# Two-layer hybrid diffusion block on one core: each token mixer starts inside the last group of the mixer before it

## The chip, the cores and the metric

One core of a Trainium2 chip runs the whole program. The metric is device time in microseconds (us), the median of several executions.

## The reference, cut to what matters

Two layers act on 512 latent tokens and, in layer 0, on 256 context tokens as well, each token 1024 wide, in fp32. One layer computes:

```python
hl = rmsnorm(x, ln1_g[l]) * (1.0 + sc1) + sh1
hc = rmsnorm(xc, ln1_g[l]) * (1.0 + csc1) + csh1
zl, zc = hl @ w_in[l], hc @ w_in[l]        # one wide projection, split by columns
ya = hyena_branch(hy)                      # two long convolutions, by DFT matrices here
yb = global_attention_branch(ga)           # 4 heads of 128, qk-norm, axial rotary
yc = mlstm_branch(ml)                      # 4 heads, forward and backward
yd = window_attention_branch(wa)           # 8 heads of 64, band of 128, sink logits
acc = sum(sigmoid(gate[n]) * (ys[n] @ w_up[n]) for n in range(4))
x = x + g1 * (acc @ w_out)
x = x + g2 * sq_relu_mlp(h2, w1, b1, w2, b2)
```

The four branches read the same normed input and do not read each other. Only the sum of the four joins them.

## The kernel before, in words

**Number format.** Most products are done as three fp32r matmuls: an operand is split into a high part H (a cast on ScalarE) and a low part L (a subtraction on VectorE or GpSimd), and H·H, H·L and L·H are summed in PSUM. `load` brings one weight tile of 256 KB (512 rows of 128 columns) from HBM and splits it. Two of these make one projection column block: 24 matmuls of 512 columns, and 24 more of 256 columns where the context tokens take part.

**An order written out by hand.** The program text is made by Python generators ("strands"). A strand emits instructions and yields an estimate of how long it has to wait. `run` steps the main strand when its wait is over on a modelled clock `clk`, and between steps calls `fill_step`, which emits work from three queues: `side` (the Hyena filter spectra), `mods` (blocks of the modulation matrix) and `jobs` (sigmoid gates, `gate_units`, and the gated sum, `merge_units`). This work is called filler below. Every TensorE instruction is chained to the one emitted before it, so TensorE executes exactly in the order of emission; the order on the other engines is settled when the program is built, and a tile that finds no free buffer makes its first writer wait.

**The mixers.** In each layer, four strands run one after the other, each with a `run` of its own: `wa` (window attention), `ga` (global attention), `ml` (mLSTM), `hy` (Hyena). `intake` loads the weights of a list of column blocks, always one block ahead, and projects them; a flag `busy` lets only one intake be under way. A mixer starts with an intake of its first blocks (`wa`, `ga`: k, v and a first q; `ml`: its gate columns, then v, k and q of head 0; `hy`: three channel blocks), has four groups (heads or channel blocks), and within a group `pipe` keeps two steps alive; the intake for the next group is one of the items of the pipe. The last group has no such item. After a mixer, its `merge_units` are added to `jobs`; after `wa`, the loop first empties `side`.

**Buffers.** 17 SBUF tiles of 768 columns (`slot`), 8 of 1024 columns (`big`), 4 raw weight tiles, 6 split weight tiles of each kind. PSUM has three pairs: `p2` (1024 columns, two banks each; projections, scores, transposes), `p1` (512; small sums and outputs), `m` (512; the filler's own). `wa` holds for its whole last group V, four key tiles and two query tiles, and per step one tile for the probabilities and one for their transpose; the output takes two. `ga`'s first intake keeps three tiles for k, one for v and three for q until its norm and rotary (`prep`) are done.

**After the four mixers** `drain` empties the queues, then `last_merge` adds the Hyena branch, followed by the output projection and the MLP.

Of the kernel before, what the change touches and what calls it, by code (L numbers as in the profile page):

```python
# [25 lines left out]
SEQ = 512  # L26
CTX = 256
# [4 lines left out]
HY0, GA0, ML0, WA0, GT0 = 0, 1536, 2560, 4624, 5392  # L32
LAT = (0, SEQ)
CTXS = (SEQ, CTX)
NT, NS = 17, 8
LEAD = 7.0
PACE = {"hy0": 6, "hy1": 2.55, "mlp": 7}
WT = {"wa1": 4.0, "wa2": 1.4, "waq": 6.0, "wak": 3.0, "gap": 3.19, "gaq": 2.0, "ga1": 4.0, "ga2": 1.4, "gas": 6.0,
# [67 lines left out]
def hybrid_block(ctx: ExitStack, tc: tile.TileContext, I, C, out, dbg=None, stop=None):  # L106
# [10 lines left out]
    cnt, ph, clk, last, busy = [0], ["pre"], [0.0], [None], [False]  # L117
# [32 lines left out]
    def acc_tile(segs, filler=False):  # L150

        if filler:
            return [(t0, n, pf1()[:, :n]) for t0, n in segs]
        w, t = span(segs), p2()
        return [(w.start, w.stop - w.start, t[:, w])]
# [189 lines left out]
    def span(segs):  # L345
        a = min(s[0] for s in segs)
        b = max(s[0] + s[1] for s in segs)
        return slice(a, b)
# [359 lines left out]
    def hview(hH, hL):  # L708
        return lambda k: (hH[:, k, :], hL[:, k, :])

    def intake(l, specs, mov, paired=None):

        def weights(col, segs, permute, use):
            w = I["w_in"][l][:, col : col + P]
            return [load((lambda raw, x=x: permute(raw, x)) if permute else wcols(w, x)) for x in range(2)]

        while busy[0]:
            yield 0.4
        busy[0] = True
        ahead = weights(*specs[0])  # L720
        if paired:
            second = weights(*specs[1])
        yield LEAD
        for i, (col, segs, permute, use) in enumerate(specs):
            W = ahead
            if paired and i < 2:
                if i == 0:
                    Ws = W, second
                    ps2 = [acc_tile(t[1]) for t in specs[:2]]
                    yield from paired(ps2, Ws, mov)  # L730
                else:
                    ahead = weights(*specs[2])
                use(ps2[i])
                continue
            if i + 1 < len(specs):
                ahead = weights(*specs[i + 1])
            ps = acc_tile(segs)
            yield from proj(ps, W, mov)
            use(ps)
        busy[0] = False  # L740
# [50 lines left out]
    def window_branch(l, vt, mov, segs, ymk, late, paired):  # L791
# [80 lines left out]
        def next_query(j):  # L872
            yield from intake(l, [query(j)], mov)
            yield WT["waq"]
            Q[j] = stack_q(rope2(*Q[j], segs), segs)
# [53 lines left out]
        for j in range(4):  # L929
            items = [step(j, i, r) for i in range(nblk) for r in range(2)]  # L930
            if j < 3:
                items.insert(3, next_query(j + 1))
            yield from pipe(items)

    def global_branch(l, vt, mov, segs, ymk):
# [59 lines left out]
        def rows(kv, h):  # L995

            yield from intake(l, (key(kv) if kv is not None else []) + [query(h)], mov)
            if kv is not None:
                s, sq, sw, v = K[kv]
                pt = tokens_major(v, full)  # L1000
                V = slot(name="gV")
                nc.vector.tensor_copy(V[:, :TOT], pt[:, :TOT])
                kH, kL, _ = yield from prep(s, sq, sw, full, True)
                K[kv] = kH, kL, V
            else:
                yield WT["gaq"]
            Q[h] = yield from prep(*Q[h], segs, False)
# [41 lines left out]
        for h in range(4):  # L1049
            items = [step(h, i) for i in range(nblk)]  # L1050
            if h < 3:
                items.insert(2, rows(1 if h == 1 else None, h + 1))
            yield from pipe(items)

    def mlstm_branch(l, vt, mov, segs, ymk):
# [10 lines left out]
        for x in range(2):  # L1066
            H, L = (t.rearrange("p k n -> p (k n)") for t in whalf())
            nc.gpsimd.memset(H.bitcast(F32), 0.0)
            nc.gpsimd.memset(L.bitcast(F32), 0.0)
            quad = lambda t: t.rearrange("p (k g c) -> p k g c", k=4, g=4)  # L1070
            low(quad(H)[:, :, :, 0:4], quad(L)[:, :, :, 0:4], quad(raw[:, x * 64 : x * 64 + 64]), heng=nc.vector)
            W.append([t.rearrange("p (k n) -> p k n", k=4) for t in (H, L)])
        pg = acc_tile(full)
        yield from proj(pg, W, mov)
        gb = tiny(8, "gb")
# [239 lines left out]
        yield from pipe([columns(), head(0)])  # L1315
        yield WT["mlh"]
        for h in range(4):
            yield from pipe([mix(h)] + ([head(h + 1)] if h < 3 else []))

    def hyena_branch(l, vt, mov, segs, ymk, near_end):  # L1320
        tabs = {}
        for n in (SEQ, CTX) if CTXS in segs else (SEQ,):
            kt, nb = n // 256, n // P
            fw = [big(name="dft") for _ in range(2)] if n == SEQ else None
            t = big(name="dft") if n == CTX else None
            tv = []
            for j, nm in enumerate(("ap", "am", "tp", "tm")):
                k = kt if j < 2 else nb
                c = n if j < 2 else n // 2
                if n == SEQ:  # L1330
                    b_ = big(name="dft") if j >= 2 else fw[j]
                    v = b_.rearrange("p (k n) -> p k n", k=k)
                else:
                    v = t[:, j * 256 : (j + 1) * 256].rearrange("p (k n) -> p k n", k=k)
                nc.sync.dma_start(v, C[f"{nm}{n}"].rearrange("(k p) n -> p k n", p=P))
                tv.append(v)
            tabs[n] = tv
        w = span(segs)
        U = {}

# [87 lines left out]
                yield WT["hy5"]  # L1428
                U[ct].append(None)

        yield from inputs(0)
        yield WT["hy5"]
        if len(segs) > 1:
            for ct in range(4):
# [49 lines left out]
    def pipe(gens, depth=2):  # L1484

        it, live, more = iter(gens), [], True
        while True:
            while more and len(live) < depth:
                g = next(it, None)
                if g is None:  # L1490
                    more = False
                else:
                    live.append([g, clk[0]])
            if not live:
                return
            e = next((e for e in live if e[1] <= clk[0] + 1e-6), None)
            if e is None:
                yield min(e[1] for e in live) - clk[0]
                continue
            try:  # L1500
                e[1] = next(e[0]) + clk[0]
            except StopIteration:
                live.remove(e)
            yield 0.0
# [26 lines left out]
    def next_fill():  # L1531

        if cur[0] is not None:
            return cur[1]
        return min([q[0].after for q in queues()] + [1e9])
# [11 lines left out]
    def fill_step():  # L1547
# [19 lines left out]
        ph[0] = mine  # L1567
        return True

    def run(lab, gen, pace=0):  # L1570

        ready, i = clk[0], 0
        while True:
            if ready <= clk[0] + 1e-6:
                if WT["eager"] and cur[0] is None and cur[2] is None and side and side[0].after <= clk[0]:
                    fill_step()
                ph[0] = lab
                try:
                    ready = next(gen) + clk[0]
                except StopIteration:  # L1580
                    return
                i += 1
                if pace and i % pace == 0:
                    fill_step()
            elif not fill_step():
                clk[0] = min(ready, max(next_fill(), clk[0] + 0.05))
# [330 lines left out]
    first = []  # L1917
# [26 lines left out]
    for l in range(DEPTH):  # L1944
# [38 lines left out]

        if l == 0:
            first_jobs()
        yds = {}
        for n, lab, branch in ((3, "wa", window_branch), (1, "ga", global_branch), (2, "ml", mlstm_branch),
                               (0, "hy", hyena_branch)):
            yds[n], mk = ymaker(l, n, segs)
            res, extra = [], []  # L1990
            if n == 3:
                extra = [late, by_pieces(full, hdone) if l else by_halves]
            elif n == 0:
                merge = last_merge(l, 0, gd[0], segs, yds[0], res)
                extra = [lambda: next(merge)]
            strand = branch(l, vt, mov, segs, mk, *extra)
            if l and n == 3:
                strand = pipe(before + [then(hdone, full, first_jobs), strand], 9)
            run(f"{lab}{l}", strand, pace=PACE.get(f"{lab}{l}", 0))
            if n == 3 and l == 0:  # L2000
                vturn(False)
            if n == 2 and l == 0:
                vloads(True, nc.sync)
                vloads(False, nc.sync)
            if n == 0 and l == 0:
                vturn1(True)
                vturn1(False)
            while n == 3 and side:
                if not fill_step():
                    clk[0] = max(next_fill(), clk[0] + 0.05)  # L2010
            if n:
                jobs.extend(merge_units(l, n, mov, segs, yds[n], gd.get(n), first=n == 3))
        drain()
        sc2 = mod_scale(l, vt, 4, "ln2_g")
        run(f"mg0x{l}", merge)
# [85 lines left out]
```

## Time and profile before

| | before |
|---|---|
| time, median of 3 runs | 3291.99 us (3285.04 to 3303.0) |
| the profiled execution: its own time | 3282.8 us |
| its span, from first to last instruction | 3281.0 us |
| TensorE matmuls busy (PE) | 3087.7 us, 94% |
| weight loads busy (PEld) | 80% |
| VectorE, ScalarE, GpSimd busy (DVE, ACT, POOL) | 41%, 35%, 42% |
| mean granted TensorE clock, as a share of full speed | 0.976 |

PE is the TensorE matmul queue, PEld its weight loads, SP the queue that issues the transfers. A busy time counts every instruction from start to end; where PE's busy time is close to the window's width, TensorE was never without a matmul. In the view by windows, the width less PE's busy time is its idle time.

### The profile page before, as it was taken

The page shows a single profiled execution, that of the slowest core. Times are in us where ns is not written, and L with a number is a line of the kernel's source. Part 1 is how long each engine was busy: PE and PEld are TensorE (multiplying, and loading weights), DVE is VectorE, ACT ScalarE, POOL GpSimd, SP SyncE. Part 2 cuts the span into 40 slices and gives each one's busy share as a digit, 9 for nine tenths or more (in the row PEclk, how much of TensorE's full clock was granted, in tenths as well). Part 3 has the DMA queues.
Part 4 walks back from the last instruction along what each step waited for, and adds up shares of the span by engine and source line. Part 5 has one row for each costly group of instructions (what it writes and reads, how often), then busy time and mean ns, then how long its engine had stood idle before and what let it go on. Part 6 is the DMA issues. An engine that isn't in the chain of part 4 may idle for free. (4 is left out here: it accounts for less than half of the span.)

```text
span 3281.0 us, 48633 instructions
## 1 busy us (share of the span) xinstructions
PE 3087.7 (94%) x18344; PEld 2614.1 (80%) x18344; DVE 1337.5 (41%) x2892; ACT 1135.7 (35%) x2137; POOL 1384.8 (42%) x1206
## 2 busy tenths in 40 slices
PE   7888989899999999999999997989998999999999
PEld 5777778788888888888888876777777788788887
DVE  6544422454444454511221265434354434442223
ACT  5435423234332122422222254333333432243333
POOL 4523332324344453443333355233333455555553
PEclk8999999999999999999999988999999999999999
DMA  8343443333243456222222334544343343823332
GB/s 269 102 115 114 124 147 94 106 101 95 78 147 92 137 173 198 68 78 75 71 74 75 95 99 121 145 136 113 100 113 98 104 137 116 273 84 97 97 97 81
DMA packets 556922, 380.24 MB, mean 116 GB/s; under 512 B 45177, under 2 KB 503870, under 8 KB 556688
## 3 DMA queue, kind: packets, MB, share of 16 engines
q1 hardware_dynamic: 556056, 376.98, 38.5%
q8 instruction: 145, 2.38, 0.3%
q14 instruction: 89, 0.73, 0.1%
q10 hardware_dynamic: 632, 0.16, 0.0%
HBM read 307.52 MB, written 63.75 MB: 113 GB/s over the span
## 5 line engine op out<-in xcount | busy, mean ns | idle before, releaser
L177 POOL TENSOR_TENSOR mlp__wL<-mlp__raw,mlp__wH 128x512 fp32r<-128x512 f32 x268 | 353.6, 1321 | 457.8 <-ACT mlp__wH L193 324.3
L193 ACT CAST mlp__wH<-mlp__raw 128x512 fp32r<-128x512 f32 x268 | 166.2, 621 | 505.3 <-PE mlp__p L215 340.6
L177 POOL TENSOR_TENSOR gt__wL<-gt__raw,gt__wH 128x512 fp32r<-128x512 f32 x128 | 167.4, 1313 | 240.1 <-ACT gt__wH L193 208.7
L215 PE MATMUL mlp__p<-out__hH,mlp__wH 128*128 128x512 f32 (+1 forms) x760 | 259.5, 353 | 0.5 <-ACT out__hH L518 0.5
L215 PE MATMUL mlp__p<-out__hL,mlp__wH 128*128 128x512 f32 (+1 forms) x760 | 256.5, 352 | 2.0 <-POOL out__hL L516 1.8
L180 DVE SCALAR_TENSOR_TENSOR mlp__x<-mlp__p,modT,mlp__x 128x512 f32<-128x512 f32 (+1 forms) x169 | 106.3, 657 | 338.3 <-PE mlp__p L215 332.1
L215 PE MATMUL mlp__p<-mlp__y,mlp__wH 128*128 128x512 f32 (+1 forms) x672 | 231.9, 356 | 0.0
L215 PE MATMUL mlp__p<-mlp__aL,mlp__wH 128*128 128x512 f32 (+1 forms) x672 | 231.2, 355 | 0.0
L177 DVE TENSOR_TENSOR mlp__aL<-mlp__mq,mlp__y 128x768 fp32r<-128x768 f32 (+1 forms) x64 | 82.4, 1287 | 304.3 <-ACT mlp__y L193 304.1
L215 PE MATMUL gt__m<-mod__hH,gt__wH 128*128 128x512 f32 (+1 forms) x512 | 172.1, 352 | 7.6 <-ACT mod__g L423 3.4
L215 PE MATMUL mlp__p<-out__hH,mlp__wL 128*128 128x512 f32 (+1 forms) x760 | 177.2, 350 | 0.0
L215 PE MATMUL gt__m<-mod__hL,gt__wH 128*128 128x512 f32 (+1 forms) x512 | 166.6, 341 | 0.0
L177 POOL TENSOR_TENSOR ml__wL<-ml__raw,ml__wH 128x512 fp32r<-128x512 f32 x64 | 83.9, 1311 | 189.8 <-ACT ml__wH L193 173.1
L215 PEld LDWEIGHTS mlp__p<-out__hH,mlp__wH 128*128 128x128 f32 x760 | 144.0, 189 | 22.0 <-issue 2.2
L215 PEld LDWEIGHTS mlp__p<-out__hL,mlp__wH 128*128 128x128 f32 x760 | 143.4, 190 | 22.4 <-POOL out__hL L516 2.2
L215 PE MATMUL mlp__p<-mlp__y,mlp__wL 128*128 128x512 f32 (+1 forms) x672 | 155.8, 354 | 0.0
L215 PEld LDWEIGHTS mlp__p<-out__hH,mlp__wL 128*128 128x128 f32 x760 | 130.0, 190 | 18.8
L215 PEld LDWEIGHTS mlp__p<-mlp__y,mlp__wH 128*128 128x128 f32 x672 | 126.8, 189 | 19.9 <-issue 2.2
L215 PEld LDWEIGHTS mlp__p<-mlp__aL,mlp__wH 128*128 128x128 f32 x672 | 127.1, 189 | 18.0
L193 ACT CAST gt__wH<-gt__raw 128x512 fp32r<-128x512 f32 x128 | 79.0, 619 | 173.1 <-DMA gt__raw<-in_w_in_dram 108.0
L215 PEld LDWEIGHTS mlp__p<-mlp__y,mlp__wL 128*128 128x128 f32 x672 | 115.0, 189 | 17.6
L215 PEld LDWEIGHTS gt__m<-mod__hH,gt__wH 128*128 128x128 f32 x512 | 98.3, 192 | 20.9 <-ACT mod__g L423 4.9
(574 smaller groups left out, 7915.5 us busy)
## 6 DMA issues: line engine op xcount, KB each, us to landing
mlp__raw<-in_mlp_w_dram SPq DMA_DIRECT2D x240, 256.0 KB
mod__raw<-in_w_mod_dram SPq DMA_DIRECT2D x160, 256.0 KB
gt__raw<-in_w_in_dram SPq DMA_DIRECT2D x128, 256.0 KB
ml__raw<-in_w_in_dram SPq DMA_DIRECT2D x64, 256.0 KB
hy__raw<-in_w_in_dram SPq DMA_DIRECT2D x48, 256.0 KB
spec<-spec__kk SPq DMA_DIRECT2D x80, 128.0 KB
ga__raw<-in_w_in_dram SPq DMA_DIRECT2D x32, 256.0 KB
hy__spec<-spec SPq DMA_DIRECT2D x16, 512.0 KB
```

The source lines that it names most:

```text
L177: (eng or nc.vector).tensor_tensor(o, a, b, op)
L180: nc.vector.scalar_tensor_tensor(o, a, s, b, op0, op1)
L193: nc.scalar.copy(H, src)
L215: in_order(nc.tensor.matmul(ps, lhsT=a, rhs=b, start=start, stop=stop_), cost)
```

## The change: what it does, and the diff

The four strands of a layer become members of one outer `pipe` of depth 4, in the old order of priority, under a single `run`. Each strand (`mixer`, wrapped in `staged`) polls every 0.3 us of modelled time until its name is in `near`. The mixer before it adds that name by the item `hint`: `wa` as the fourth item of its last group (`NEAR = 3`), `ga` as the third of its last group, `ml` at the start of its last head. From then on both strands are stepped, the earlier one first. `ml` gets a modelled wait (`LEAD`, 7.0) between the load of its gate weights and their projection. Hyena's DFT tables are no longer requested at the start of its strand but by `late_tables`, once `ml` has ended. The emptying of `side` after `wa` becomes a wait of `wa`'s strand alone. The pace at which `run` forces a filler step goes by the mixer that was stepped last. What the fillers load, and how far ahead, stays as it was.

```diff
-NT, NS = 17, 8
+NT, NS, NEAR = 17, 8, 3
...
+    def hint(n):
+
+        near.add(n)
+        yield 0.0
...  (window attention, then global attention, then mLSTM)
             if j < 3:
                 items.insert(3, next_query(j + 1))
+            else:
+                items.insert(NEAR, hint("ga"))
...
             if h < 3:
                 items.insert(2, rows(1 if h == 1 else None, h + 1))
+            else:
+                items.insert(2, hint("ml"))
...
+        yield LEAD
         pg = acc_tile(full)
         yield from proj(pg, W, mov)
...
-            yield from pipe([mix(h)] + ([head(h + 1)] if h < 3 else []))
+            yield from pipe([mix(h)] + ([head(h + 1)] if h < 3 else [hint("hy")]))
...  (Hyena: the loop over the tables becomes tables(n))
+        def late_tables():
+            while "ml" not in ended:
+                yield 0.3
+            for n in (SEQ, CTX) if CTXS in segs else (SEQ,):
+                tables(n)
...
-        yield from inputs(0)
+        yield from pipe([inputs(0), late_tables()])
...
+    def staged(lab, n, strand, first=None):
+
+        while n not in near:
+            yield 0.3
+        if first:
+            first()
+        while True:
+            ph[0] = lab
+            try:
+                lat = next(strand)
+            except StopIteration:
+                break
+            if begun_[-1:] != [lab]:
+                begun_.append(lab)
+            yield lat
...
+                every = pace() if callable(pace) else pace
+                if every and i % every == 0:
...  (the loop over the four mixers becomes mixer(n, lab, branch))
             strand = branch(l, vt, mov, segs, mk, *extra)
             if l and n == 3:
                 strand = pipe(before + [then(hdone, full, first_jobs), strand], 9)
-            run(f"{lab}{l}", strand, pace=PACE.get(f"{lab}{l}", 0))
-            if n == 3 and l == 0:
-                vturn(False)
+            yield from staged(f"{lab}{l}", lab, strand, (lambda: vturn(False)) if n == 1 and l == 0 else None)
+            while n == 3 and side:
+                yield 0.2
...
-            while n == 3 and side:
-                if not fill_step():
-                    clk[0] = max(next_fill(), clk[0] + 0.05)
             if n:
-                jobs.extend(merge_units(l, n, mov, segs, yds[n], gd.get(n), first=n == 3))
+                jobs.extend(merge_units(l, n, mov, segs, yd, gd.get(n), first=n == 3))
+            ended.add(lab)
+
+        res = []
+        run("", pipe([mixer(*a) for a in ((3, "wa", window_branch), (1, "ga", global_branch), (2, "ml", mlstm_branch),
+                                          (0, "hy", hyena_branch))], 4), pace=lambda: PACE.get(begun_[-1], 0))
```

## Rows read from the trace of the kernel before

**Rows 1.** The page, part 1: span, busy time of each engine.

```profile
span 3281.0 us, 48633 instructions
PE 3087.7 (94%) x18344; PEld 2614.1 (80%) x18344; DVE 1337.5 (41%) x2892; ACT 1135.7 (35%) x2137; POOL 1384.8 (42%) x1206
```

**Rows 2.** Windows, PE alone: stretch and width, busy (count), clock, DMA share, GB/s.

```profile
80.00:1240.00 1160.00, 1084.70 (x7051) 0.98 0.39 118
1240.00:1860.00 620.00, 618.57 (x3684) 0.99 0.28 85
2080.00:2840.00 760.00, 711.34 (x4219) 0.98 0.43 127
```

**Rows 3.** Windows, PE alone: the six hand-overs, layer 0, then layer 1.

```profile
408.00:442.00 34.00, 25.47 (x146) 0.85 0.72 229
686.00:740.00 54.00, 50.29 (x275) 0.97 0.44 136
955.00:1010.00 55.00, 55.00 (x327) 1.00 0.43 124
2206.00:2250.00 44.00, 43.08 (x262) 1.00 0.47 136
2408.00:2470.00 62.00, 57.24 (x321) 0.97 0.36 98
2630.00:2690.00 60.00, 59.33 (x291) 0.97 0.53 155
```

**Rows 4.** Timeline of PE, first hand-over: start, us, instruction, [idle before <-releaser].

```profile
418.02 0.65 PE L217 MATMUL mod__m<-mod__raw,scp 128*32 128x128 f32 x16 [1.86 <-ACT spec__od L679]
419.53 0.63 PE L215 MATMUL ga__p<-mod__hH,ga__wH 128*128 128x512 f32 x1
425.16 0.40 PE L215 MATMUL ga__p<-mod__hL,ga__wH 128*128 128x512 f32 x1
434.99 0.80 PE L215 MATMUL ga__p<-mod__hH,ga__wH 128*128 128x512 f32 x1 [6.19 <-ACT ga__wH L193]
```

**Rows 5.** Timeline of SP, the same hand-over.

```profile
420.95 4.05 SPq L1620 DMA_DIRECT2D mg3x__y<-yd  x7
426.70 1.63 SPq L315 DMA_DIRECT2D ga__raw<-in_w_in_dram  x2
```

**Rows 6.** Windows, PE alone: middle and later groups of global attention.

```profile
484.00:545.00 61.00, 59.74 (x425) 1.00 0.36 106
545.00:610.00 65.00, 58.56 (x395) 0.95 0.29 83
610.00:686.00 76.00, 73.04 (x525) 1.00 0.33 93
2250.00:2310.00 60.00, 53.35 (x356) 0.94 0.43 124
2310.00:2350.00 40.00, 37.39 (x238) 1.00 0.29 80
```

**Rows 7.** Timeline of PE: waits inside groups of global and of window attention.

```profile
587.35 1.54 PE L227 MATMUL ga__p<-ident,ga__gp 128*128 128x128 f32 x6 [4.24 <-DVE ga__gp L172]
589.94 2.93 PE L215 MATMUL ga__p<-ga__gpt,ga__gV 128*128 128x128 f32 x12 [1.05 <-DVE ga__gpt L1036]
...
2149.14 0.38 PE L215 MATMUL wa__p<-wa__wkH,wa__wqX 128*128 128x256 f32 x1 [1.30 <-DVE wa__wst L894]
...
2153.76 1.30 PE L227 MATMUL wa__p<-ident,wa__wp 128*128 128x128 f32 x5 [3.88 <-DVE wa__wp L172]
```

**Rows 8.** Timeline of SP (tables), and the tables' tile view: ns, first and last start.

```profile
940.90 0.38 SPq L1335 DMA_DIRECT2D hy__dft<-const_ap_dram  x1
...
974.72 0.34 SPq L1460 DMA_DIRECT2D yd<-ml__yH  x1
...
L215 PEld LDWEIGHTS hy__p<-hy__fF,hy__dft x576: 186/192/337, 1012.5 to 2817.0; 128*128 128x128 f32 x192
```

**Rows 9.** Windows, PE alone: the end of the mixers in both layers.

```profile
1200.00:1240.00 40.00, 36.37 (x212) 0.96 0.71 235
2800.00:2840.00 40.00, 38.47 (x176) 0.96 0.90 301
```

More of the change, by code (lines that the diff above doesn't have):

```diff
@@ L1317, in mlstm_branch, with tables @@
         for h in range(4):
-            yield from pipe([mix(h)] + ([head(h + 1)] if h < 3 else []))
+            yield from pipe([mix(h)] + ([head(h + 1)] if h < 3 else [hint("hy")]))
     def hyena_branch(l, vt, mov, segs, ymk, near_end):
         tabs = {}
-        for n in (SEQ, CTX) if CTXS in segs else (SEQ,):
+        def tables(n):
             kt, nb = n // 256, n // P
@@ L1568, in fill_step @@
         return True
+    def staged(lab, n, strand, first=None):
[12 more added lines that the diff above has]
+            yield lat
+    near, ended, begun_ = set(), set(), [""]
     def run(lab, gen, pace=0):
@@ L1582, in run @@
                 i += 1
-                if pace and i % pace == 0:
+                every = pace() if callable(pace) else pace
+                if every and i % every == 0:
                     fill_step()
@@ L1985, in hybrid_block, with mixer @@
             first_jobs()
[L1986 to L1990, printed above, removed]
+        near.clear()
+        ended.clear()
+        near.add("wa")
+        merges, strands = [], []
+        def mixer(n, lab, branch):
+            yd, mk = ymaker(l, n, segs)
+            extra = []
             if n == 3:
@@ L1993, in hybrid_block @@
             elif n == 0:
-                merge = last_merge(l, 0, gd[0], segs, yds[0], res)
-                extra = [lambda: next(merge)]
+                merges.append(last_merge(l, 0, gd[0], segs, yd, res))
+                extra = [lambda: next(merges[0])]
             strand = branch(l, vt, mov, segs, mk, *extra)
@@ L2007, in hybrid_block @@
                 vturn1(False)
-            while n == 3 and side:
-                if not fill_step():
-                    clk[0] = max(next_fill(), clk[0] + 0.05)
             if n:
-                jobs.extend(merge_units(l, n, mov, segs, yds[n], gd.get(n), first=n == 3))
+                jobs.extend(merge_units(l, n, mov, segs, yd, gd.get(n), first=n == 3))
[3 more added lines that the diff above has]
+                                          (0, "hy", hyena_branch))], 4), pace=lambda: PACE.get(begun_[-1], 0))
+        merge = merges[0]
         drain()
```

## The prediction

> **What bounds the kernel now.** I read the first part of the page, then the span cut into windows, then the six places where one mixer hands over to the next, and there the timelines of PE and SP. TensorE is the bound: its matmuls are busy 94% of the span, and no other engine passes 42% beside the weight loads [rows 1]. So time can be won only where PE is idle or where its clock is down. The windows say where that is: the MLP of layer 0 has 1.4 us of idle time in 620 us, while the mixers of layer 0 (80 to 1240) have 1160 - 1084.7 = 75.3 us and those of layer 1 (2080 to 2840) 760 - 711.3 = 48.7 us [rows 2]. The reader is to see that the change aims at the right stretch, 124 us of idle time, but that the hand-overs are only a part of it.
>
> How large a part, the six windows tell [rows 3]. Layer 0, wa to ga: 34 - 25.47 = 8.5 us idle. ga to ml: 3.7. ml to hy: none. Layer 1: 0.9, 4.8 and 0.7. The sum is 18.6 us. The fillers already cover five of the six hand-overs; the first one is the exception. There the timeline shows two gaps, 1.86 us behind the emptying of the spectra and 6.19 us before the third half of ga's first weights is split [rows 4]. SP shows why: seven of the eight loads of window attention's output, 384 KB each, were issued from 420.95 on, and the weights only at 426.70 [rows 5]. After each gap the clock is at its lower level, 1.2 GHz: the same 512-column matmul takes 0.63 us at 419.53 and 0.40 us at 425.16 [rows 4]. By the start times some 8 and 11 matmuls of that size ran so, 0.43 us apart instead of 0.23: 19 x 0.2 = 3.8 us on top.
>
> **The change part by part.**
>
> *Removed.* The hand-overs as such, since the next mixer's intake is emitted inside the last group. At most all of [rows 3] goes, with the clock: 8.5 + 3.8 in the first; 3.7 and about 1 of clock at ga to ml; 4.8 and about 1 at the same place in layer 1 (both at 0.97, so 54 x 0.03 and 62 x 0.03 = 1.6 and 1.9 us of lost cycles, of which part fell into the gaps); 0.9 and 0.7. Sum 12.3 + 4.7 + 0.9 + 5.8 + 0.7 = 24.4 us. The lower bound of this term is zero, as the waits inside mLSTM's column chain may only move.
>
> *Moved.* The intakes stand earlier, so the fillers that covered the last groups stand later. No matmul is added or saved, and PE's total work stays. The fillers left over at the end are drained with PE nearly full: at the end of layer 1 PE is idle 1.5 us in 40, with the DMA engines 90% busy; in layer 0 3.6 us in 40 [rows 9]. If one more stretch of 40 us of merges is drained per layer at that rate instead of beside Hyena, it costs 2 x 1.5 to 2 x 3.6 us less what they would have cost elsewhere; the idle rate of the mixers of layer 0 is 75.3 / 1160 x 40 = 2.6 us in 40. The difference is within 2 us, and I enter zero. The burst of loads of [rows 5] is also moved, to where the leftover gates are done and ga already has its weights a block ahead; I enter no cost, but with that cover gone it is the 6.2 us of [rows 4] again.
>
> *Hyena's tables.* They are requested after `ml` in program order. In the trace they were issued at 940.90, 34 us ahead of mLSTM's last output store at 974.72, as soon as large tiles came free, and first used at 1012.5 [rows 8]. The order on SP is thus set by readiness and free tiles, not by the place in the text, and I expect the same here: cost zero. If not, 2.25 MB in layer 0 and 2 MB in layer 1 at the 301 GB/s of [rows 9] are 7.5 and 6.6 us, all before the first transform. Queued behind them on SP would be the next channel block's weights.
>
> *ml's added wait and the polls* emit nothing. The wait only lets others be emitted before the gate projection: zero, covered by ga's steps. The pace of forced fillers in Hyena counts steps of the outer pipe, so it comes somewhat more often. PE is full there and the work exists anyway: zero.
>
> *Added: pressure on buffers.* Two steps of the old group and one intake now live together, on two `p2` pairs and 17 small tiles. By the code, window attention's last group holds 7 tiles, 2 for the output and about 4 for its steps, and ga's intake 7 before any is given back: 20 against 17. Then somebody waits, and since PE's order is fixed, PE waits as well and no filler can slip in. The trace has the nearest case: the group of global attention which takes in k, v and q beside its steps. In layer 0 it is idle 65 - 58.56 = 6.4 us, where its neighbours have 1.3 in 61 and 3.0 in 76 [rows 6]; its waits are 4.24 and 1.05 us on VectorE's chain, and 18 matmuls behind them at half clock took 1.54 and 2.93 us, about 2.2 us too long [rows 7]. That is 4.3 + 2.2 = 6.5 us more than its neighbours. In layer 1 it is 6.65 us in 60 against 2.6 in 40, so 2.8 more, and with the clock at 0.94 about 1.6 on top: 4.4. The change makes two such places per layer, wa with ga's intake and ga with ml's. Mixing with a head's intake exists in `ml` already, so Hyena's adds none. Upper bound by these rows: 2 x 6.5 + 2 x 4.4 = 21.8 us; lower bound zero, if waiting steps find the tiles free in time. I take the middle, 11 us, since in the neighbours the intake of one block costs nearly nothing and in this group that of three costs all.
>
> The Trainium skill, in "Perfetto Trace Analysis" under "Identifying Performance Opportunities", says both things about this change: interleaving stretches with different limits may help, and the same gap repeating on the engine that should be full can mean that SBUF or PSUM has no room for the next tile. Rows 6 and 7 agree with the second in kind, though the trace does not name the missing buffer. By the first alone the sum would be -24, by the second alone a loss, which is the slower rival below.
>
> *Sum.* -24.4 + 11 = -13.4, say -13 us. The profiled execution of 3282.8 us would become 3270; it stands 9.2 us under the median of the runs, so I forecast 3292 - 13 = 3279 us. Against the 0.5% (16.5 us) which a measurement of this kernel can tell from no change, that is no difference.
>
> **The rivals.**
>
> *A, clean overlap.* The tiles suffice or the waits fall where fillers stand ahead; all of 24 us goes, and less half-clock time or better cover inside the last groups gives some more. For it: the idle time in the last groups is small and random. Against: the tile count. Time 3292 - 24 = 3268, down to 3257 with a few us inside the groups. Clearly faster.
>
> *B, window attention starves (slower).* Where ga's intake holds its seven tiles, each half-step of window attention runs alone, and PE stands for its softmax chain. Place: the last group of wa, where 9 half-steps remain in layer 0 and 5 in layer 1. Price: the wait before the transposes at 2153.76, 3.88 us, which followed a wait for a scores buffer at 2149.14 [rows 7], in a moment when query preparation ran beside the steps. All 14 so: 54 us, net 54 - 24 = +30, or 3322. It decides from 24.4 / 3.88 = 6.3 uncovered half-steps on; from 11 on the loss passes 0.5%. For it: 20 tiles for 17. Against: three of four groups already hold a query's intake, and there such waits are rare.
>
> *C, no effect.* The pressure costs its upper bound of 22 us and eats the gain, or the waits of the hand-overs merely move along: 3290 ± 8.
>
> *D, late tables.* Both layers wait 7.5 + 6.6 = 14 us for the tables; with the forecast's -13 this gives about 3293. Against it stands [rows 8].
>
> **How the numbers follow.** Forecast (-3 to -21 us) 0.42; A 0.22; C 0.12; D 0.06; B 0.18. Faster by over 0.5%: A and a third of the forecast, 0.36. Slower: most of B and a little of D's sum with B, 0.20. The rest, 0.44, within 0.5%. The likeliest case alone spans 3271 to 3289. The range reaches down to A, 3257, and a little less for the spread of the runs (3285 to 3303, some 9 us either way, of which I take 4): 3253. Up it takes B to about two thirds of its price, +20: 3312.
>
> **What would show it.** Right: in the profile after, no PE wait over 2 us in the first hand-over; ga's projections (`ga__p`) start before wa's last transposes; more merges stand behind Hyena's last transform; waits of 1 to 4 us, with a dip of the clock, inside the last group of wa or ga. Wrong by A: the last groups show no such waits and idle time in the mixers falls from 124 us by 20 or more. Wrong by B: PE waits on `wa__wp` or on score buffers many times between ga's projections. Wrong by D: a PE wait on the tables' transfers at Hyena's first transform. A change of the idle time in the MLP or at the start would mean that my account of what the change touches is incomplete.

## The result and the profile after

The change made the kernel slower. The median of four executions is 3334.14 us (3332.76 to 3341.42) against 3291.89 us before; the ratio is 1.0131, interval [1.0112, 1.015]. I had forecast 3279 us, at most 3312.

The page, first part, of the changed kernel; it answers to [rows 1]:

```profile
span 3333.3 us, 48652 instructions
PE 3115.1 (93%) x18344; PEld 2632.4 (79%) x18344; DVE 1331.2 (40%) x2892; ACT 1134.2 (34%) x2137; POOL 1385.2 (42%) x1206
```

The same 18344 matmuls take 52 us more. Windows of the changed kernel (stretch, width, PE busy, clock, DMA share, GB/s), cut near the first matmul of the last merge, as those of [rows 2] are; the last line is the first hand-over of [rows 3]:

```profile
80.00:1262.00 1182.00, 1095.67 (x7030) 0.97 0.39 116
1262.00:1882.00 620.00, 617.88 (x3667) 0.99 0.28 84
...
2104.00:2890.00 786.00, 724.37 (x4225) 0.97 0.43 123
408.00:442.00 34.00, 30.59 (x198) 0.95 0.30 90
```

The MLP is untouched: 2.1 us idle in 620, before 1.4. The mixers of layer 0 have 1182 - 1095.67 = 86.3 us of idle time (75.3 before), those of layer 1 61.6 (48.7 before). They also stay busy 11 and 13 us longer on the same work; the granted clock is 0.97 there, where it was 0.98. Together that is 48 us, nearly all of the loss.

The hand-over itself went nearly as intended. Timeline of PE in the changed kernel:

```profile
378.25 0.50 PE L215 MATMUL ga__p<-mod__hH,ga__wH 128*128 128x512 f32 x1 [0.56 <-DVE wa__wst L899]
...
384.24 0.63 PE L227 MATMUL wa__p<-ident,wa__wp 128*128 128x128 f32 x4 [1.01 <-DVE wa__wpt L913]
...
432.27 1.10 PE L215 MATMUL spec__m<-spec__ab,spec__fs 128*128 128x256 f32 x4 [3.41 <-DVE ga__rt L177]
```

Global attention projects from 378 on, among window attention's transposes, and the waits of 1.86 and 6.19 us of [rows 4] are gone. One new wait stands in the same window, 3.41 us before a matmul of the spectra, ended by VectorE's rotary for global attention. So where did 50 us go? The tile view gives the first and the last start of the last merge's matmuls. In the kernel before, a row not yet shown, and then in the changed kernel:

```profile
L215 PE MATMUL mg0x__p<-hy__y,hy__wH x36: 278/389/398, 1238.1 to 2838.1; 128*128 128x512 f32 x24, 128*128 128x256 f32 x12
```

```profile
L215 PE MATMUL mg0x__p<-hy__y,hy__wH x36: 277/389/397, 1261.8 to 2887.9; 128*128 128x512 f32 x24, 128*128 128x256 f32 x12
```

The last merge begins 24 us later in layer 0 and 50 us later in layer 1, so each layer gives away about 25 us ahead of it. Hyena's last matmul, however, comes earlier in layer 0 than before (1181 instead of 1232). Between it and the last merge stands the drained filler: 80.5 us of it in layer 0 (5.7 before) and 45.4 us in layer 1 (11.1 before). Windows of the changed kernel, with all engines (PE, PEld, DVE, ACT, POOL); the first and the last lie inside the two drains, the second ends 18 us behind the first drain:

```profile
1200.00:1240.00 40.00, 32.40 (x153) 25.77 (x153) 5.46 (x10) 4.60 (x8) 15.96 (x11) 0.87 0.78 257
1240.00:1280.00 40.00, 33.99 (x186) 29.35 (x185) 11.56 (x16) 6.54 (x10) 17.71 (x13) 0.96 0.90 290
2840.00:2880.00 40.00, 34.14 (x129) 25.09 (x128) 7.98 (x12) 8.00 (x13) 20.10 (x16) 0.91 0.75 236
```

No engine is full, and the DMA engines are busiest: 236 to 290 GB/s where the mixers average 116 to 123. In each window PE is idle for 6 to 8 us, where [rows 9] had 3.6 and 1.5. What PE waits for there, in the view of waits (total, times, longest), then in its timeline, then SP's, all of the changed kernel:

```profile
PE mg2x__m L215 <- DVE mg2x__g L180: 8.3, 4, 3.9
PE mg2x__m L215 <- DMA mg2x__y<-yd: 5.3, 8, 2.5
```

```profile
1236.81 2.08 PE L215 MATMUL mg2x__m<-mg2x__y,mg2x__wH 128*128 128x512 f32 x8 [2.31 <-DVE mg2x__g L180]
...
1256.05 3.60 PE L215 MATMUL mg2x__m<-mg2x__y,mg2x__wH 128*128 128x512 f32 x8 [3.88 <-DVE mg2x__g L180]
```

```profile
1205.55 3.81 SPq L1657 DMA_DIRECT2D mg2x__y<-yd  x8
...
1225.64 0.38 SPq L1680 DMA_DIRECT2D mg2x__g<-gate  x1
1227.85 0.32 SPq L1684 DMA_DIRECT2D mg2x__g<-accd  x1
1228.23 0.42 SPq L1727 DMA_DIRECT2D mg0x__ac<-accd  x1
```

These are the eight merges of mLSTM. First the eight loads of its outputs (3 MB in layer 0) are requested at once, and every wait on them is counted. Then each merge needs its weights, a stored gate and the earlier sum, and writes the new sum: 256 + 3 x 384 KB, 1.4 MB for about 4.2 us of matmuls (33.3 us for eight, e6 below). "PE waits for VectorE" is only the nearest link. The tile view of `mg2x__m` says what VectorE itself waited for before it could empty the PSUM bank (us, times); in the kernel before, and then in the changed one:

```profile
  DMA mg2x__g<-gate: 8.9, 2
```

```profile
  DMA mg2x__g<-gate: 36.8, 8
```

**Lost time, by stage.** For every pair of neighbouring matmuls I took the time from start to start in the trace, less what a matmul on the same tiles and of the same shape takes unhindered (the 30th percentile of its intervals in the kernel before). The remainder is idle time and the time at the lower clock level in one number. Stages end with the last matmul of the mixer; "drain" runs from Hyena's last matmul to the last merge's first.

| lost, us | wa | ga | ml | hy | drain | wa | ga | ml | hy | drain |
|---|---|---|---|---|---|---|---|---|---|---|
| layer | 0 | 0 | 0 | 0 | 0 | 1 | 1 | 1 | 1 | 1 |
| before | 86.5 | 39.6 | 18.1 | 19.8 | 0.1 | 98.3 | 28.9 | 29.1 | 6.5 | 0.0 |
| after | 92.7 | 40.6 | 30.2 | 3.5 | 22.3 | 101.5 | 35.3 | 29.4 | 9.0 | 12.5 |
| e1, no overlap | 94.1 | 30.7 | 16.2 | 12.6 | 0.1 | 93.6 | 27.3 | 23.5 | 8.0 | 0.0 |

After less before: 50.1 us, of which 34.7 in the drains. One profile is good to some 4 us in a stage: window attention of layer 0 has the same order of matmuls in the kernel before and in e8, e9, e13 and e17 below, and lost 86.1 to 94.9 us.

### The profile page after: what moved, and what is told of

Same layout as the page of the kernel before. It is cut to its first block, busy times and chain, and to the rows that moved or that the text cites. A ratio compares the mean times of both kernels' runs of the same rounds, so it can differ in the third digit from the quotient of the medians.

```text
span 3333.3 us, 48652 instructions
## 1 busy us (share of the span) xinstructions
PE 3115.1 (93%) x18344; PEld 2632.4 (79%) x18344; DVE 1331.2 (40%) x2892; ACT 1134.2 (34%) x2137; POOL 1385.2 (42%) x1206
## 5 line engine op out<-in xcount | busy, mean ns | idle before, releaser
L215 PEld LDWEIGHTS mlp__p<-out__hH,mlp__wH 128*128 128x128 f32 x760 | 144.8, 191 | 22.5 <-issue 2.2
L193 ACT CAST gt__wH<-gt__raw 128x512 fp32r<-128x512 f32 x128 | 79.1, 620 | 186.6 <-DMA gt__raw<-in_w_in_dram 101.5
```

The costliest lines, as they stand in the source:

```text
L193: nc.scalar.copy(H, src)
L215: in_order(nc.tensor.matmul(ps, lhsT=a, rhs=b, start=start, stop=stop_), cost)
```

## The experiments

All times are medians, and "drain" is its length in the two layers, read from each trace. The ratio is to the kernel before as measured beside each group of experiments; its medians there lay between 3289.3 and 3292.0 us. I began with two theories: the displaced fillers cost their price when they are drained (T1), or two mixers starve each other of buffers (T2).

| run | us | ratio to before | drain, us |
|---|---|---|---|
| e1 no overlap | 3263.44 | 0.9924 [0.9902, 0.9947] | 4.3, 8.4 |
| e2 more forced filler | 3331.64 | 1.0128 [1.0106, 1.0149] | 19.3, 0.0 |
| e3 only wa to ga | 3308.48 | 1.0063 [1.0038, 1.0087] | 35.9, 23.3 |
| e4 only ml to hy | 3260.85 | 0.9924 [0.9894, 0.9954] | 24.0, 23.7 |
| e5 only ga to ml | 3270.27 | 0.9943 [0.9925, 0.996] | 22.5, 11.1 |
| e6 no overlap, merges held | 3287.61 | 0.9991 [0.998, 1.0003] | 44.4, 27.5 |
| e7 changed, fewer loads | 3311.46 | 1.0066 [1.0048, 1.0084] | 69.9, 40.2 |
| e8 before, fewer loads | 3286.27 | 0.9981 [0.9968, 0.9995] | 5.7, 11.1 |
| e9 no overlap, spectra first | 3262.87 | 0.9915 [0.99, 0.993] | 0.0, 8.4 |
| e10 no overlap, no lead | 3257.42 | 0.9896 [0.9878, 0.9914] | 8.5, 11.1 |
| e11 only wa to ga, 16 tiles | 3302.58 | 1.0033 [1.0021, 1.0045] | 34.6, 23.0 |
| e12 no overlap, 16 tiles | 3271.23 | 0.9943 [0.9925, 0.9962] | 4.3, 8.4 |
| e13 before, late tables | 3277.91 | 0.9959 [0.9945, 0.9974] | 4.3, 11.1 |
| e14 no overlap, early tables | 3257.51 | 0.9895 [0.9881, 0.991] | 4.3, 8.4 |
| e15 wa to ga, late hint | 3271.3 | 0.994 [0.9918, 0.9962] | 18.1, 8.4 |
| e16 ml to hy, no lead | 3275.27 | 0.995 [0.993, 0.997] | 23.7, 36.3 |
| e17 before, fine steps | 3272.38 | 0.9941 [0.9921, 0.9961] | 4.3, 11.1 |
| e18 no overlap, e10 and e14 | 3258.76 | 0.9905 [0.9889, 0.9921] | 8.5, 11.1 |

**e1, nothing overlapped.** All else of the change stays; a strand may start when the one before it has ended.

```diff
+OVERLAP = ()            # e3: ("ga",)   e4: ("hy",)   e5: ("ml",)
 def hint(n):
-    near.add(n)
+    if n in OVERLAP:
+        near.add(n)
...  (end of a mixer)
+            if lab in NEXT:
+                near.add(NEXT[lab])
             while n == 3 and side:
                 yield 0.2
```

> The changed kernel with the three hints disarmed: the four strands stay members of one outer pipe, with late tables, the wait in front of mLSTM's gate projection and the new pace, but each strand starts only when the one before it has ended. When the program is written out, 1 and 3 filler units are left in the queue at the end of Hyena in layers 0 and 1 (before: 1 and 4; the changed kernel: 14 and 12). Theory T1 (the fillers displaced to the end are drained against the transfers): back to the time of the kernel before, 3285 to 3300. Theory T2 (two strands at once starve each other of buffers): the same, 3285 to 3300. Rival R (the regrouping itself costs: polls, late tables, pace): stays near 3334, at least above 3315.

3263.44 us: the overlap is worth not 42 but 71 us of loss, and the rest of the change, which both theories took for neutral, gains 28. The first hand-over shows that its wait did not need an overlap to go. Windows of e1:

```profile
408.00:442.00 34.00, 34.00 (x199) 0.95 0.75 236
```

**e2, the changed kernel with more forced filler in Hyena** (`PACE` of Hyena 6 and 2.55 to 2 and 2).

> The changed kernel, all three overlaps kept, but inside Hyena a filler step is forced every 2 steps (6 and 2.55 before), so that 4 and 0 filler units are left at Hyena's end instead of 14 and 12. T1: most of the loss at the two ends comes back, 22 to 30 us: 3304 to 3312. T2: nothing changes, as the overlaps stay: 3328 to 3340. R: no change either.

3331.64 us; T1 as I had put it is wrong. The drains lost only 2.6 us instead of 34.8, but Hyena lost 13.0 and 25.4 instead of 3.5 and 9.0: 25.9 of the 32.2 us saved were handed on. What made Hyena dearer is not separated: in layer 1 the longest waits there are Hyena's own on VectorE (7.0 us), those on the merges' outputs come to 3.0.

**e3, e4 and e5, one overlap each.**

> Only the hint from window to global attention armed; 7 and 7 units left at Hyena's end. T1: loss about in proportion to the units left, (14 - 5) of (26 - 5) of 42 us: 18, so about 3310. T2: this is one of the two crowded places per layer, half of the loss: 3311 to 3315. Together with the next run it is the sum that tells: under T2 this one has nearly half of the loss and the next nothing.

> Only the hint from mLSTM to Hyena armed; 5 and 7 units left at Hyena's end. T1: (12 - 5) of 21 of 42 us: 14, so about 3306. T2: no crowded place is made here, since mixing beside an intake exists in the kernel before: 3290 to 3296.

> Only the hand-over from global attention to mLSTM is overlapped; the other two wait for the end of the mixer before, as in the run without any overlap (3263 us). 4 filler units are left when Hyena ends in each layer, against 1 and 3 without overlap. If the loss of the whole change comes only from fillers drained at the end: 3266 to 3272 us. If two mixers that share the buffers starve each other wherever they meet, as the hand-over from window to global attention suggests (+45 us by itself): 3283 us or more.

Over e1, wa to ga costs 45 us, ga to ml 7 and ml to hy gains 3, within the spread. One place makes most of the loss. All three together cost 70.7, 21 more than the sum of the three. Half of that is in the drains, with 34.8 us lost against 10.7 + 5.8 + 7.5 = 24.0. Besides, mLSTM of layer 0 loses some 30 us in each of the three traces with all overlaps (the changed kernel, e2, e7) and 15 to 17 in e1, e3, e4 and e5; why stays open. For the drains the tile view of `mg2x__y` suggests a reason; SP's line of the changed kernel (ns, first and last start):

```profile
L1657 SPq DMA_DIRECT2D mg2x__y<-yd x16: 320/382/542, 1205.6 to 2851.2; - x16
```

and that of e3:

```profile
L1660 SPq DMA_DIRECT2D mg2x__y<-yd x16: 319/382/1303, 1187.6 to 2822.1; - x16
```

With one overlap the outputs are still loaded inside Hyena (whose last matmul starts at 1211 and 2833 in e3); with all three they are loaded in the drain (Hyena's last at 1181 and 2839).

**e6, the drain without any overlap.** e1, with mLSTM's merges kept until Hyena has ended.

```diff
-                jobs.extend(merge_units(...))
+                (last_units if n == 2 else jobs).extend(merge_units(...))
...  (after the run over the mixers)
+        jobs.extend(last_units)
         drain()
```

> No overlap at all, but the eight merge units of mLSTM of each layer are kept back until Hyena has ended and then drained. If merges that run back to back are limited by their transfers: in layer 0 3 MB of outputs and eight times 1.4 MB at 290 GB/s take 49 us against 33 us of matmuls, in layer 1 10 MB take 35 us against 22 us, so some 29 us lost in the two drains, and 3290 to 3300 us instead of 3263. If the drain is costly only together with an overlap: 3263 to 3270 us.

3287.61 us, 24 more than e1. In layer 0 the drain holds just the eight merges: 33.3 us of matmuls took 44.4 us. Windows of e6:

```profile
1200.00:1240.00 40.00, 33.08 (x171) 28.31 (x170) 6.81 (x14) 4.34 (x7) 21.71 (x14) 0.91 0.92 300
```

The DMA engines are 92% busy at 300 GB/s. The drains lost 11.1 + 5.5 us, less than the 29 I had worked out, and Hyena, without the merges as cover, 3 and 8 more. So drained merges are dear by themselves, on both sides.

**e7 and e8, fewer transfers in mLSTM's merges**, in the changed kernel and in the one before:

```diff
+                    if n == 2:
+                        nc.gpsimd.memset(sg[:, w], 0.0)
+                    else:
                         nc.sync.dma_start(sg[:, w], gd[m][:, w])
...  (and the same for T["a", m], read from accd[m])
```

> The changed kernel with all its overlaps; the merges of mLSTM leave out reading the gate and the earlier sum from memory (both tiles are filled with zeros on GpSimd instead, so tiles and matmuls stay as they were). That takes 0.77 MB of 1.4 MB from a merge in layer 0, 0.5 of 1.0 MB in layer 1. If the drain is bound by transfers, most of the 35 us lost there come back: 3300 to 3312 us instead of 3334. If it is bound by tiles or by the chain behind each merge: 3328 us or more.

> The control to the run before: the kernel before with the same reads left out in mLSTM's merges. There the merges lie inside Hyena and cover its waits, so if transfers matter only in the drain, nothing changes: 3285 to 3292 us. If fewer transfers help everywhere, it gains as much as the changed kernel does.

The changed kernel gains 22.7 us, the kernel before 5.7 (3292.0 over 19 executions less 3286.27 over 10). Tiles and matmuls were the same, so some 17 us of the change's loss are these transfers (by the intervals of the three ratios, good to about 10). The trace agrees: with the same order of matmuls the drains lose 18.8 us instead of 34.8. Waits of e7 from 1170 to 1270:

```profile
PE mg2x__m L215 <- DMA mg2x__y<-yd: 5.3, 8, 1.9
```

The waits for VectorE are gone; those for the 3 MB of outputs stay, to the tenth. What is left in the drains is 11.6 and 7.2 us.

**e9 and e10, where e1's gain comes from.** e9 lets global attention begin only when `side` is empty, as before; e10 leaves out the `LEAD` before mLSTM's gate projection.

> No overlap, and global attention may begin only after the spectra's queue is empty, as in the kernel before (in the run without overlap it begins while that queue is still being emptied; 3263 us, 28 us less than the kernel before). If the gain of 28 us comes mainly from that barrier, whose 20 us window lost 11.9 us before and 2.8 us without it: 3272 to 3280 us. If it comes from order in many places: 3268 us or less.

> No overlap, and without the modelled wait between the load of mLSTM's gate weights and their projection. If that wait lets fillers cover the load and carries the rest of the gain of 28 us (4.7 and 5.8 us of hand-over in the two layers): 3270 to 3276 us. If it carries nothing: 3259 to 3267 us.

Neither carries it: 3262.87 and 3257.42 us. In e9 the 10 us in global attention of layer 0 did come back (40.9 lost instead of 30.7), yet the whole stayed the same; less was lost elsewhere in that trace.

**e11 and e12, 16 tiles instead of 17.**

> Only the hand-over from window to global attention is overlapped, with 16 tiles of 768 columns instead of 17; compared with the next run. With 17 the overlap costs 45 us. If the two mixers starve each other of these tiles, one tile less makes it dearer: 60 us or more over the next run. If tiles do not bind and the cost is that of the order in which work is emitted, it stays at 35 to 55 us.

> The control: no overlap with 16 tiles. If one mixer by itself has tiles to spare: 3260 to 3268 us, as with 17. If 17 is already tight for a single mixer: 3275 us or more.

The overlap costs 3302.58 - 3271.23 = 31 us with 16 tiles, 45 with 17. A shortage should have made it dearer. T2 falls for these tiles; more than 17 were not tried, and no other buffer was varied. Each run has TensorE's order of its partner with 17 tiles (e3, e1) and yet differs from it by -6 and +8 us, so a change of 14 us in the cost of the overlap is no finding.

**e13 and e14, the tables alone.**

> The kernel before with one edit: Hyena's tables are requested after its first loads and projections have been written out instead of at its start. The run without overlap gains 28 us on the kernel before, and neither the barrier of the spectra nor the modelled wait carries it. If the later tables carry it: 3275 us or less. If not: 3284 to 3298 us.

> The converse: no overlap, tables requested at the start of Hyena's strand as in the kernel before. If the later tables carry the gain: 3278 us or more. If it is the one run over all four strands, whose steps and polls shift where fillers are emitted: 3256 to 3270 us.

3277.91 us (11 less than before) and 3257.51 (6 less than e1): late tables help the one kernel and early ones the other. In e14 the order of all matmuls is that of e1. In e13 it differs from before only inside Hyena of layer 0, because the edit also passes Hyena's first loads through a pipe and so changes what the pace counts.

**e15, wa to ga with a late hint** (`NEAR` 12 instead of 3, behind the group's last step).

> Only the hand-over from window to global attention is overlapped, but the hint stands behind the last step of the group instead of behind the third item; 4 and 3 filler units are left at Hyena's end instead of 7 and 7. If it is the depth of the overlap that costs, because the intake then covers the group in place of fillers: 3262 to 3278 us. If any meeting of the two mixers costs the 45 us: 3295 us or more.

3271.3 us, 8 over e1. But on TensorE the two mixers no longer meet in this run: global attention's first matmul (414.8 and 2200.5) follows window attention's last (414.6 and 2199.9); only its weights are loaded earlier. In e3 the two are mixed for 38 and 19 us. So the early loads are cheap and the 45 us come with the mixing; e15 does not tell whether by the cover it uses up or by something else the two share.

**e16, the edits of e4 and e10 together.**

> The two edits that gained, together: only mLSTM to Hyena is overlapped and the modelled wait before mLSTM's gate projection is left out. If the gains add up: 3261 - 6 = 3255 us, 3250 to 3260. If the 9 filler units left in layer 1 cost what drained merges cost elsewhere: 3262 to 3270 us.

3275.27 us, the other side. Layer 1's drain is 36.3 us long and lost 11.6 us (e4: 23.7 and 4.4): the last load of mLSTM's outputs was issued at 2792.9, 4 us after the start of Hyena's last matmul (2788.8); in e4 at 2777.7, 10 us before Hyena's last matmul there.

**e17, only the stepping.** The kernel before, each strand beside a polling one:

```diff
-            run(f"{lab}{l}", strand, pace=...)
+            run(f"{lab}{l}", pipe([whole()] + ([polls()] if n else []), 4), pace=...)
```

> The kernel before with one edit: each mixer still has its own run and its old order, but its strand is stepped through an outer pipe beside a strand that polls every 0.3 us, as in the changed kernel. TensorE's order then differs from before only inside Hyena, where the pace of forced fillers counts about twice as many steps. If that carries Hyena's share of the gain (12.6 instead of 19.8 us lost there in layer 0): 3280 to 3286 us. If it carries the whole gain: 3263 to 3270 us. If nothing: 3287 to 3296 us.

3272.38 us (3260.34 to 3282.08): 17 of the 28 us. Hyena of layer 0, the only stage in which TensorE's order differs, loses 6.9 us instead of 19.8, and 10 of these 13 us lie between 1120 and 1140. A window and the waits of the kernel before, which had not been shown, and then of e17 (its waits from 1110 to 1180):

```profile
1120.00:1160.00 40.00, 34.32 (x180) 0.87 0.63 207
PE mg2x__m L215 <- DMA mg2x__y<-yd: 5.5, 7, 2.3
```

```profile
1120.00:1160.00 40.00, 39.08 (x252) 1.00 0.60 197
PE mg2x__m L215 <- DMA mg2x__y<-yd: 0.5, 1, 0.5
```

It is mLSTM's merges once more: with about twice as many steps counted, forced fillers come more often, and the first merge no longer meets its own loads.

**e18, the two edits that gained, together** (e10 and e14).

> No overlap, without the modelled wait (e10, 3257 us) and with the tables requested early (e14, 3258 us), the two edits that each gained 6 us on the run without overlap. If they add up: 3248 to 3255 us. If both only shift the order by chance, as the two gains of e16 did: 3254 to 3266 us.

3258.76 us, within the spread of both parts: these gains do not add up. It beats both kernels, the one before by 1% and the changed one by 75 us, and so do e10 and e14.

## Why the prediction was wrong, step by step

*Removed* (24.4 us at most): the waits of [rows 4] went, the 6.19 us with them, though a new one of 3.41 us came. But e1 shows 34 us busy in 34 there, so they go without an overlap too. What the overlap itself brought, at the two cheap places, is +7 and -3 us (e5, e4).

*Moved: "the difference is within 2 us, and I enter zero."* This step failed first. I priced the drained merges at the idle rate of [rows 9], 1.5 to 3.6 us in 40, but only 6 and 11 us of those windows are drain, the rest is other work in a mixture, and I left uncounted what the last merges in the queue, mLSTM's, have to move. Drained, they lost 34.7 us in the trace; held back without any overlap they cost 24 (e6); with two of their transfers taken out, the changed kernel got some 17 us more back than the one before (e7, e8). That transfers bind there is shown for about half of the drains' loss; of the other 18.8 us the waits for the outputs, 5.3 us in layer 0, are transfers too, and the rest is not assigned. My own arithmetic would have warned me: 1.4 MB per 4.2 us of matmuls is some 335 GB/s, more than the 301 GB/s that [rows 9] show as the fullest stretch.

*Added: pressure on buffers, 11 us (0 to 21.8).* The places that I priced stayed clean. Windows of the changed kernel over the end of window attention's last groups, where global attention's intake runs among them:

```profile
376.00:417.00 41.00, 35.62 (x236) 1.00 0.12 33
2185.00:2235.00 50.00, 43.35 (x318) 1.00 0.40 112
```

No wait in them is longer than 1.4 us, and the granted clock is 1.00; in the kernel before, the last 41 and 50 us of window attention had 4.8 and 3.3 us of idle time, at clocks of 1.00 and 0.94. The waits of 1 to 4 us with a dip of the clock, which this term stood for, did not come. One place of my four, wa to ga, does cost 45 us (e3), but mostly behind the crowded stretch: by lost time some 11 of these lie in the drains, 18 in global attention after window attention has ended, and the rest is scattered. In global attention of layer 1 PE waits 8.9 us for the transposed probabilities from VectorE (e1: 3.2); in layer 0 one filler of the spectra waits 3.4 us for global attention's rotary. The 768-column tiles are not the reason (e11, e12), and the cost goes when the two mixers are not mixed (e15). My reading is that the projections of the intake, which PE could run alone without loss, are spent as cover in a group that gates had covered before, and the gates are then drained; that part is argued, not shown. The Trainium skill, "Perfetto Trace Analysis", "Identifying Performance Opportunities", names missing room in SBUF or PSUM as a possible cause of repeated gaps. It was right to weigh, but here it was not the cause as far as the 768-column tiles go.

*The pace of forced fillers: zero.* Wrong in the other direction: finer stepping alone gains 17 us (e17). The rest of e1's 28 us is not settled: by stages it is 9 us in global attention of layer 0, 2 and 6 in mLSTM, but e9 gave the first back and stayed as fast.

*mLSTM's added wait* (zero): the run without it is 6 us faster (e10). *Hyena's tables* (zero): later ones gain 11 us in one kernel, where the pace changed with them (e13), and earlier ones gain 6 in the other (e14). Kernels with TensorE's order unchanged differ by 6 to 8 us (last section), so nothing here speaks against these zeros. Rival D is out: in the changed kernel's trace PE never waits for a table.

*The rivals.* The time fell on B's side, by none of its mechanism: window attention did not starve (92.7 us lost in layer 0, against 86.1 to 94.9 in the kernels with the old order). Of the signs that I had listed as "right", two were seen: global attention's projections start early, and "more merges stand behind Hyena's last transform"; it is just to this sign that I had given no price. Two were not: a wait of over 2 us (3.41) does stand in the first hand-over, and the last groups of wa and ga show no waits with a dip of the clock, which should have told me that the loss lies elsewhere.

## What to carry to other kernels

When steps are overlapped by hand, ask not only which gaps close but which filler is left over, and price that very filler by its bytes per microsecond of TensorE work against the fullest transfer rate that the trace shows; work that only moves is not free. Cover is finite: if my reading holds, an overlap that lets dense projections hide a chain's waits leaves the filler that hid them to be run where nothing needs hiding. And before a change is judged as one thing, run it with its main switch off: here that alone turned 1.3% of loss into 0.8% of gain.

## What the runs showed of the hardware that I had not expected

In the drain of the changed kernel the same eight matmuls of 512 columns took 2.08 us after a wait of 2.31 us and 3.60 after one of 3.88. In e6 they took 2.08 us after 0.61, 3.47 after 3.09, and after 3.01 2.71, with the four behind them at 1.91 instead of 1.07. In the changed kernel the granted clock was 1.00 from 1236 to 1239 and 0.58 from 1256 to 1260: behind each of the three longest of these waits a part of the matmuls ran at the lower of the two clock levels. So in a stretch bound by transfers the clock made a long wait dearer by another 1.4 to 1.7 us.

And kernels whose matmuls come in exactly the same order still differ: e14 from e1 by 6 us with only the place of some loads changed, e12 from e1 by 8 with one tile less (these were not run side by side). Stages in the same order differ by up to 9 us from one profile to another. A small gain of re-ordering was not additive in either of the two trials (e16, e18).
